# A two-layer decoder on one core: probabilities scaled in two steps, and half of the gate products as 7 block products in place of 8

## The chip, the cores and the metric

One core of a Trainium2 chip runs the whole program. The metric is the device time of one execution in microseconds (us); lower is better. The engines are called as in the profile: PE is TensorE (matmuls; its weight loads are listed apart as PEld), DVE is VectorE, ACT is ScalarE, POOL is GpSimd, SP is SyncE, which here only issues DMAs.

## What is computed

The program is a decoder of two layers on 512 rows of 1024 features, in float32. Each layer has an input projection, four attentions of four heads each (MoBA, FoX, MLA, dilated), an output projection, and a SwiGLU feed-forward part (FFN) of 2816 columns, with RMS norms around both. Cut to what the change touches:

```python
p = jax.nn.softmax(sc, axis=-1)
o = jnp.einsum('bhqk,bhkd->bhqd', p.astype(v.dtype), v)
...
f = jax.nn.silu(jnp.einsum('bsd,df->bsf', h, w_gate[l])) * jnp.einsum('bsd,df->bsf', h, w_up[l])
f = jnp.einsum('bsf,fd->bsd', f, w_down[l])
x = x + rmsnorm(f, g_post_ffn[l])
```

## The kernel before

**Precision.** A float32 operand goes to PE as a high part and a low part. ACT rounds the high part off (a cast), DVE subtracts it to get the low part; both together are called a split here. `mm3` (lines 196 to 199) makes one product of such operands with three matmuls, on lines 197, 198 and 199.

**Attention.** `attend` (line 438) is a generator for one unit: one head and the query tiles `qa` to `qb`, of 128 rows each. There are 20 units per layer, 12 with four query tiles (FoX, MLA, MoBA) and 8 with two (dilated). For each tile PE makes the scores (L454), DVE adds the mask and finds the row's extreme (L457), ACT takes the exponential and sums the row into `den` (L459, an ACTIVATE and then a short instruction that reads the sum out). After the last tile DVE inverts all sums (L462), and POOL multiplies each tile by its inverse (L465), from the shortest (128 columns) to the longest (512). Then PE transposes the scaled blocks (L474): the first bank that is filled takes one block of every query tile, so a unit with four tiles fills it only when the last tile is scaled. ACT and DVE split the transposed blocks (L476, L477), and PE multiplies them by the values (L482, L483). `weave` (line 397) interleaves the units with projection work, and begins the scores of the next unit before the current one is finished.

**FFN.** `ffn` (line 800) works through 22 column blocks of 128. Blocks 0 and 1 are done apart. From block 2 on, a gate block is 8 products of 128 by 128 weights with 512 columns of the transposed input, so 24 matmuls of 512 columns (`block`, L811), followed by SiLU on ACT (L928). At every odd block the up projection of two blocks is made by `two_blocks` (L891), which cuts weights and input in 2 by 2 blocks and forms the result from 7 products of blocks in place of 8 (Strassen's scheme in Winograd's form). Each of the 7 is 4 by 3 matmuls of 256 columns. The sums of input blocks are made once per layer (L843 to L866); the sums of weight blocks are made per pair: 4 `combine` (L882), 7 splits (L876, L877), 2 copies of a product out of PSUM (L901, L904) and 7 `add` (L894), all but the copies and casts on DVE. The up result goes to two scratch tiles, and DVE multiplies it onto the gate (L936).

**Order and buffers.** Every engine runs its instructions in order. The order is laid out when the program is built, by priority of program order and by a planner's costs; at run time engines wait for one another on semaphores. Split weights have 6 buffers (`WSPL`), raw weights 5 (`WRAW`), the sums of weight blocks 4 (tag `temp`). The 7 products of a pair take PSUM banks from four pools: 3 banks `ps_mm`, 2 `ps_s`, 2 `ps_t`, 1 `ps_o`. After the last pair the down projection (`ps_d`) fills all 8 banks.

Of the kernel before, what the change touches and what calls it, by code (L numbers as in the profile page):

```python
# [13 lines left out]
ALU = mybir.AluOpType  # L14
PSUM = bass.MemoryType.PSUM

P = 128
# [64 lines left out]
def decoder(ctx, tc, x, positions, w_in, b_forget, g_mla_q, w_mla_q_up, g_mla_kv, w_mla_kv_up,  # L82
            w_out, g_pre_mix, g_post_mix, w_gate, w_up, w_down, g_pre_ffn, g_post_ffn, consts, out):
    nc = tc.nc
# [10 lines left out]
    def bank(pool, name):  # L95
        return pool.tile([P, 512], F32, name=name, tag=pool.name)
# [10 lines left out]
    def H(name):  # L107
        return keep.tile([P, 512], F32, name=name, tag="part", bufs=NPART)
# [165 lines left out]
    def mixing(l, h_in, in_slots, out_slots, w_first):  # L274
# [110 lines left out]
        def attention(e0, tag, passes, vt, bias, spans, outer, more=None):  # L385
            units = [(h, sp) for sp in spans for h in range(4)] if outer else [(h, sp) for h in range(4) for sp in spans]
            return [(attend(e0, tag, h, sp[0], sp[1], passes, vt, bias, more), sum(sp) * (sp[1] - sp[0]) + sp[1], lambda h=h: h in passes)
                    for h, sp in units]
# [49 lines left out]
        def attend(e0, tag, h, qa, qb, passes, vt, bias, more):  # L438
# [4 lines left out]
            den = small.tile([P, nq], F32, name="den", tag="den", bufs=4)  # L443
            pr = keep.tile([P, PRW], F32, name="pr", tag="pr", bufs=2)
            offs = {}
            off = 0
            for qt in range(qa, qb):
# [5 lines left out]
                for i, (a, b) in enumerate(terms):  # L453
                    nc.tensor.matmul(ps[:, 0:w], a if a.shape[-1] == P else a[:, qt * P:(qt + 1) * P], b[:, 0:w],  # L454
                                     start=i == 0, stop=i == n - 1)
                p = pr[:, off:off + nk]
                nc.vector.tensor_tensor_reduce(p, ps[:, 0:nk], bias(h, qt, p), scale=-1.0, scalar=3e38,  # L457
                                               op0=ALU.add, op1=ALU.min, accum_out=neg[:, qt:qt + 1])
                nc.scalar.activation(p, p, AF.Exp, bias=neg[:, qt:qt + 1], scale=-1.0, accum_out=den[:, qt - qa:qt - qa + 1])  # L459
                offs[qt] = off  # L460
                off += nk
            nc.vector.reciprocal(den, den)  # L462
            for qt in range(qa, qb):
                p = pr[:, offs[qt]:offs[qt] + (qt + 1) * P]
                nc.gpsimd.tensor_scalar(p, p, den[:, qt - qa:qt - qa + 1], 1.0, op0=ALU.mult, op1=ALU.mult)  # L465
            yield
            ncol = (qb - qa) * P
            po = bank(ps_o, "ps_o")
# [331 lines left out]
    def ffn(l, xt, h, turns, f_slots, after):  # L800
        fq = []
# [4 lines left out]
        def w_of(src, j, into=(None, None)):  # L806
            cs = slice(j * P, (j + 1) * P)
            return [weights(src[l, 4 * i * P:4 * (i + 1) * P, cs].rearrange("(k p) c -> p k c", p=P), [4, P], into=into[i])
                    for i in range(2)]

        def block(ps, w, hs):  # L811
            for k in range(KD):
                hi, lo = w[k // 4]
                mm3(ps[:, hs], hi[:, k % 4, :], lo[:, k % 4, :], h[0][k // 4][:, k % 4, hs], h[1][k // 4][:, k % 4, hs],
                    k == 0, k == KD - 1)
# [52 lines left out]
        def raw_of(src, j, i):  # L868
            raw = wp.tile([P, 4, P], F32, name="wraw", tag="wraw", bufs=WRAW)
            nc.sync.dma_start(raw, src[l, 4 * i * P:4 * (i + 1) * P, j * P:(j + 1) * P].rearrange("(k p) c -> p k c", p=P))  # L870
            return raw

        def split_w(raw):
            hi = wp.tile([P, 4, P], F32R, name="whi", tag="whi", bufs=WSPL)
            lo = wp.tile([P, 4, P], F32R, name="wlo", tag="wlo", bufs=WSPL)
            nc.scalar.copy(hi, raw)  # L876
            nc.vector.tensor_tensor(lo, raw, f32(hi), op=ALU.subtract)  # L877
            return hi, lo

        def combine(a, b, op):  # L880
            s = T(F32, "wsum").rearrange("p (k c) -> p k c", c=P)
            nc.vector.tensor_tensor(s, a, b, op=op)  # L882
            return s

        def product(pool, w, n):
            ps = bank(pool, "ps_7")[:, 0:256]
            for k in range(4):
                mm3(ps, w[0][:, k, :], w[1][:, k, :], ops[n][0][k], ops[n][1][k], k == 0, k == 3)
            return ps

        def two_blocks(src, j, d1, d2):  # L891

            def add(to, a, b):
                nc.vector.tensor_tensor(to, a, b, op=ALU.add)  # L894

            c11, c12, c21, c22 = [d[:, s] for d in (d1, d2) for s in half]
            a11 = raw_of(src, j, 0)
            a21, a22 = raw_of(src, j + 1, 0), raw_of(src, j + 1, 1)
            a12 = raw_of(src, j, 1)
            p1 = product(ps_mm, split_w(a11), "11")  # L900
            nc.scalar.copy(c12, p1)  # L901
            s1 = combine(a21, a22, ALU.add)
            p5 = product(ps_s, split_w(s1), "T1")
            nc.scalar.copy(c22, p5)  # L904
            p2 = product(ps_o, split_w(a12), "21")
            add(c11, p2, c12)
            s2 = combine(s1, a11, ALU.subtract)
            p6 = product(ps_mm, split_w(s2), "T2")
            add(c12, p6, c12)
            s3 = combine(a11, a21, ALU.subtract)  # L910
            p7 = product(ps_t, split_w(s3), "T3")
            add(c21, p7, c12)
            s4 = combine(a12, s2, ALU.subtract)
            add(c12, c12, c22)
            add(c22, c22, c21)
            p3 = product(ps_s, split_w(s4), "22")
            add(c12, p3, c12)
            p4 = product(ps_t, split_w(a22), "T4")
            add(c21, p4, c21)

        for j in range(KF):
            if j < 2:
                (pg, _), (pu, _) = halves[2 * j:2 * j + 2]
            else:
                wg, pg = w_of(w_gate, j), bank(ps_mm, "ps_g")
                block(pg, wg, slice(0, 512))
            f = fq[j]
            nc.scalar.activation(f, pg, AF.Silu)  # L928
            if j < 2:
                nc.vector.tensor_tensor(f, f, pu, op=ALU.mult)  # L930
            elif j % 2 == 1:
                u = H("u1"), H("u2")
                two_blocks(w_up, j - 1, *u)
                for i in range(2):
                    f = fq[j - 1 + i]
                    nc.vector.tensor_tensor(f, f, u[i], op=ALU.mult)  # L936
# [53 lines left out]
    for c in range(2):  # L990
        pg = bank(ps_s, "gain")
# [5 lines left out]
    with tc.manual_schedule(engines={mybir.EngineType.Activation, mybir.EngineType.DVE, mybir.EngineType.Pool}):  # L997

        st, tr = {}, {}
        for o in "s0 a0 w0 w1 t0 s1 w2 w3 a1 s2 t1 a2 s3 t2 a3 t3".split():  # L1000
            t = int(o[1])
# [10 lines left out]
    for l in range(depth):  # L1012
        pool_share[0] = SHARE_MIX
        xt, h, turns = mixing(l, h, set_a, set_b, w_first if l == 0 else None)
        nxt = []

        def after(t):
            dst = out[0] if l + 1 == depth else x_mid[l]
            for c in range(2):
                nc.sync.dma_start(dst[t * P:(t + 1) * P, 512 * c:512 * c + 512], xt[t][c])  # L1020
            if l + 1 < depth:
                if not nxt:
                    nxt.append(gain(g_pre_mix, l + 1))
                    nxt.append(new_h(set_b))
                pre_norm(t, xt[t], nxt[0], nxt[1])

        ffn(l, xt, h, turns, set_a, after)
        if nxt:
            h = nxt[1]
        set_a, set_b = set_b, set_a  # L1030
# [21 lines left out]
```

## Time and profile before

| what | us |
|---|---|
| runs of the kernel before: median of three (lowest, highest) | 1266.09 (1265.72, 1267.85) |
| the profiled execution: its own time | 1268.2 |
| its span, first to last instruction | 1266.4 |
| PE busy in the span | 1228.6 (97%) |
| DVE busy | 821.4 (65%) |
| ACT busy | 646.4 (51%) |
| POOL busy | 225.5 (18%) |

The span is the time from the first instruction to the last; the profiled execution's own time holds 1.8 us more. In a row of the timeline the first number is the start, the second the duration; matmuls are pipelined, so what a matmul costs in a dense stream is the step from its start to the next start and not its listed duration. A bracket at the end of a row tells how long the engine was idle before it and what ended that.

### The profile page before, as it was taken

Reading aid. Unit: us, or ns where it says so; the run is one execution under the profiler, and the core shown is the slowest. Engines: PE = TensorE matmul, PEld = TensorE weight load, DVE = VectorE, ACT = ScalarE, POOL = GpSimd, SP = SyncE. Lnnn points to the kernel's source line nnn. Section 1 sums busy time; section 2 is a strip of 40 time slices with the busy share of each in tenths; the row PEclk is TensorE's granted clock in tenths of the full one; section 3 lists DMA queues with packets and bytes.
Section 4 is the critical chain, followed back from the end, with each engine's and each line's share of the span. In section 5 each row is a group of like instructions: output and inputs, shape, how many; then the busy total and the mean of one; then the engine's idle time right before and its main releaser. Section 6 shows DMA issues by size and latency. Waiting matters only on the chain.

```text
span 1266.4 us, 19777 instructions
## 1 busy us (share of the span) xinstructions
PE 1228.6 (97%) x7044; PEld 1063.4 (84%) x7044; DVE 821.4 (65%) x1621; ACT 646.4 (51%) x1403; POOL 225.5 (18%) x305
## 2 busy tenths in 40 slices
PE   8999999999999999999999999999899999999998
PEld 7878877779989898888788788778798989898886
DVE  6876866787766666533466668676787666674334
ACT  6676756754434344422456767667553434353332
POOL 3223334443000000000131324433430000000001
PEclk9999999989999999999999999999999999999999
DMA  7221241521433333433342222324224333334331
GB/s 230 72 60 42 66 116 55 172 68 34 127 99 107 93 109 92 125 100 100 125 117 73 59 56 70 100 88 137 68 64 126 95 108 97 105 100 123 94 93 75
DMA packets 158054, 121.60 MB, mean 96 GB/s; under 512 B 9090, under 2 KB 133122, under 8 KB 157956
## 3 DMA queue, kind: packets, MB, share of 16 engines
q1 hardware_dynamic: 151908, 111.55, 30.3%
q10 hardware_dynamic: 6048, 8.80, 2.6%
q8 instruction: 55, 0.90, 0.3%
q14 instruction: 43, 0.35, 0.1%
HBM read 111.93 MB, written 4.19 MB: 92 GB/s over the span
## 4 chain that ended last, share of the span: by engine, by line
PE 75%; DVE 4%; ACT 2%; POOL 2%; issue 2%; DMA 1%; DVEq 0%; POOLq 0%; ACTq 0%; SPq 0%
PE ps_g L198 6%; PE ps_g L197 6%; PE ps_g L199 6%; PE ps_d L197 6%; PE ps_d L199 6%; PE ps_d L198 6%; PE ps L197 5%; PE ps L199 5%; PE ps L198 5%; PE ps_s L454 2%; PE ps_out L199 2%; PE pT L474 2%; PE ps_out L198 2%; PE ps_out L197 2%; PE ps_qk L197 2%; PE ps_qk L198 2%
## 5 line engine op out<-in xcount | busy, mean ns | idle before, releaser
L173 DVE TENSOR_TENSOR wlo<-wraw,whi 128x512 fp32r<-128x512 f32 x249 | 179.9, 729 | 149.7 <-ACT whi L168 144.8
L168 ACT CAST whi<-wraw 128x512 fp32r<-128x512 f32 x268 | 163.9, 620 | 213.2 <-PE ps_d L199 121.0
L198 PE MATMUL ps_g<-h,whi 128*128 128x512 f32 (+1 forms) x384 | 144.2, 376 | 5.0 <-DVE h L231 5.0
L197 PE MATMUL ps_g<-h,whi 128*128 128x512 f32 (+1 forms) x384 | 143.9, 375 | 1.4 <-ACT h L231 1.2
L199 PE MATMUL ps_g<-h,wlo 128*128 128x512 f32 (+1 forms) x384 | 143.6, 374 | 0.0
L876 ACT CAST whi<-wsum 128x512 fp32r<-128x512 f32 x80 | 49.7, 622 | 149.4 <-PE ps_g L198 71.9
L240 POOL TENSOR_SCALAR rstd<-ssp 128x1 f32<-128x1 f32 x16 | 6.9, 433 | 647.8 <-ACT jk L236 647.7
L465 POOL TENSOR_SCALAR pr<-pr,den 128x128 f32<-128x128 f32 (+3 forms) x128 | 78.1, 629 | 192.1 <-DVE den L462 188.6
L197 PE MATMUL ps_d<-whi,fh 128*128 128x512 f32 x288 | 112.2, 390 | 0.0
L199 PE MATMUL ps_d<-whi,fl 128*128 128x512 f32 x288 | 112.1, 389 | 0.0
L198 PE MATMUL ps_d<-wlo,fh 128*128 128x512 f32 x288 | 112.0, 389 | 0.0
L877 DVE TENSOR_TENSOR wlo<-wsum,whi 128x512 fp32r<-128x512 f32 x80 | 54.9, 690 | 83.0 <-ACT whi L876 83.0
L197 PE MATMUL ps<-sum,whi 128*128 128x256 f32 x320 | 90.2, 282 | 0.0
L198 PE MATMUL ps<-sum,whi 128*128 128x256 f32 x320 | 90.1, 282 | 0.0
L199 PE MATMUL ps<-sum,wlo 128*128 128x256 f32 x320 | 90.1, 281 | 0.0
L198 PEld LDWEIGHTS ps_g<-h,whi 128*128 128x128 f32 x384 | 73.1, 190 | 18.0 <-DVE h L231 6.2
L197 PEld LDWEIGHTS ps_g<-h,whi 128*128 128x128 f32 x384 | 73.1, 190 | 14.5 <-ACT h L231 2.7
L199 PEld LDWEIGHTS ps_g<-h,wlo 128*128 128x128 f32 x384 | 73.2, 191 | 12.6
L197 PE MATMUL ps_qk<-h,whi 128*128 128x512 f32 x192 | 76.8, 400 | 0.0
L199 PE MATMUL ps_qk<-h,wlo 128*128 128x512 f32 x192 | 75.7, 394 | 0.0
L198 PE MATMUL ps_qk<-h,whi 128*128 128x512 f32 x192 | 75.7, 394 | 0.0
L459 ACT ACTIVATE pr<-pr,neg 128x128 f32<-128x128 f32 (+3 forms) x128 | 71.5, 560 | 5.9 <-DVE neg L457 4.9
(312 smaller groups left out, 3335.2 us busy)
## 6 DMA issues: line engine op xcount, KB each, us to landing
wraw<-in_w_gate_dram SPq DMA_DIRECT2D x88, 256.0 KB, 3.4
wraw<-in_w_up_dram SPq DMA_DIRECT2D x88, 256.0 KB, 3.1
wraw<-in_w_down_dram SPq DMA_DIRECT2D x88, 256.0 KB, 2.8
wraw<-in_w_in_dram SPq DMA_DIRECT2D x72, 256.0 KB, 3.0
wraw<-in_w_out_dram SPq DMA_DIRECT2D x32, 256.0 KB, 2.9
xt<-in_x_dram SPq DMA_DIRECT2D x16, 256.0 KB, 4.4
rope_b<-rope_a ACTq DMA_DIRECT2D x64, 64.0 KB, 2.0
wraw<-in_w_in_dram SPq DMA_DIRECT2D x16, 178.0 KB, 3.6
```

The costliest lines, as they stand in the source:

```text
L168: nc.scalar.copy(hi, raw)
L173: nc.vector.tensor_tensor(lo, raw, f32(hi), op=ALU.subtract)
L197: nc.tensor.matmul(ps, a_hi, b_hi, start=start, stop=False)
L198: nc.tensor.matmul(ps, a_hi, b_lo, start=False, stop=False)
L199: last_mm[0] = nc.tensor.matmul(ps, a_lo, b_hi, start=False, stop=stop)
L240: nc.gpsimd.tensor_scalar(r, ss[:, 0:1], ss[:, 1:2], EPS, op0=ALU.add, op1=ALU.add)
L454: nc.tensor.matmul(ps[:, 0:w], a if a.shape[-1] == P else a[:, qt * P:(qt + 1) * P], b[:, 0:w], start=i == 0, stop=i == n - 1)
L459: nc.scalar.activation(p, p, AF.Exp, bias=neg[:, qt:qt + 1], scale=-1.0, accum_out=den[:, qt - qa:qt - qa + 1])
L465: nc.gpsimd.tensor_scalar(p, p, den[:, qt - qa:qt - qa + 1], 1.0, op0=ALU.mult, op1=ALU.mult)
L474: nc.tensor.transpose(pt[:, i * P:(i + 1) * P], pr[:, offs[qt] + kt * P:offs[qt] + (kt + 1) * P], ident)
L876: nc.scalar.copy(hi, raw)
L877: nc.vector.tensor_tensor(lo, raw, f32(hi), op=ALU.subtract)
```

## The change

Two edits. In `attend` the inverse and the scaling are done in two steps: after the exponential of the last but one tile for all tiles so far, and after that of the last tile for the last one. In `ffn` the gate blocks of the pairs that begin at 4, 8, 12, 16 and 20, so 5 of the 10 pairs of a layer, are made by `two_blocks`, straight into the tiles `fq[j]` and `fq[j + 1]`, where SiLU then works in place.

```diff
@@ attend
                 offs[qt] = off
                 off += nk
-            nc.vector.reciprocal(den, den)
-            for qt in range(qa, qb):
-                p = pr[:, offs[qt]:offs[qt] + (qt + 1) * P]
-                nc.gpsimd.tensor_scalar(p, p, den[:, qt - qa:qt - qa + 1], 1.0, op0=ALU.mult, op1=ALU.mult)
+
+                if qt >= qb - 2:
+                    new = range(qa, qt + 1) if qt == qb - 2 else [qt]
+                    d = den[:, new[0] - qa:qt - qa + 1]
+                    nc.vector.reciprocal(d, d)
+                    for t in new:
+                        p = pr[:, offs[t]:offs[t] + (t + 1) * P]
+                        nc.gpsimd.tensor_scalar(p, p, den[:, t - qa:t - qa + 1], 1.0, op0=ALU.mult, op1=ALU.mult)
             yield
@@ ffn
             if j < 2:
                 (pg, _), (pu, _) = halves[2 * j:2 * j + 2]
+            elif j - j % 2 in (4, 8, 12, 16, 20):
+                if j % 2 == 0:
+                    two_blocks(w_gate, j, fq[j], fq[j + 1])
+                pg = fq[j]
             else:
                 wg, pg = w_of(w_gate, j), bank(ps_mm, "ps_g")
                 block(pg, wg, slice(0, 512))
```

## Rows read from the trace of the kernel before

**Rows 1.** The page: span and busy time of the engines.

```profile
span 1266.4 us, 19777 instructions
PE 1228.6 (97%) x7044; PEld 1063.4 (84%) x7044; DVE 821.4 (65%) x1621; ACT 646.4 (51%) x1403; POOL 225.5 (18%) x305
```

**Rows 2.** Busy time by stretch: attention of layer 0, gate and up of both layers.

```profile
core 0: us, PE busy (x) PEld busy (x) DVE busy (x) ACT busy (x) POOL busy (x), PEclk, DMA share, GB/s
110.00:160.00 50.00, 47.77 (x311) 41.56 (x309) 38.69 (x88) 35.48 (x84) 19.93 (x25) 1.00 0.28 77
306.00:515.10 209.10, 209.10 (x1322) 190.24 (x1321) 144.69 (x253) 88.40 (x160) 4.23 (x3) 1.00 0.36 103
935.00:1140.00 205.00, 205.00 (x1303) 186.83 (x1303) 141.84 (x249) 87.73 (x158) 2.27 (x2) 1.00 0.36 102
```

**Rows 3.** Timeline of PE where gate (ps_g) and up (ps) change over.

```profile
316.93 0.28 PE L197 MATMUL ps<-h,whi 128*128 128x256 f32 x1
...
326.94 0.39 PE L197 MATMUL ps_g<-h,whi 128*128 128x512 f32 x1
...
337.84 0.28 PE L197 MATMUL ps<-h,whi 128*128 128x256 f32 x1
```

**Rows 4.** Timeline of DVE where it works without a pause.

```profile
367.55 0.42 DVE L894 TENSOR_TENSOR u<-u 128x256 f32<-128x256 f32 x1
367.88 0.42 DVE L894 TENSOR_TENSOR u<-ps,u 128x256 f32<-128x256 f32 x1
368.21 0.68 DVE L877 TENSOR_TENSOR wlo<-wraw,whi 128x512 fp32r<-128x512 f32 x1
368.82 0.68 DVE L936 TENSOR_TENSOR f<-f,u 128x512 f32<-128x512 f32 x1
369.42 0.41 DVE L894 TENSOR_TENSOR u<-ps,u 128x256 f32<-128x256 f32 x1
369.75 0.68 DVE L882 TENSOR_TENSOR wsum<-wraw 128x512 f32<-128x512 f32 x1
```

**Rows 5.** Busy time in one stretch, columns as in rows 2.

```profile
323.80:326.94 3.14, 3.14 (x29) 3.14 (x28) 3.11 (x8) 1.35 (x3) 0.00 (x0) 1.00 0.88 243
```

**Rows 6.** Waits in gate and up of layer 0: total us, times, longest.

```profile
ACT whi L876 <- PE ps_g L198: 38.6, 25, 2.1
DVE wlo L173 <- ACT whi L168: 6.7, 9, 0.8
DVE u L894 <- PE ps L199: 4.5, 24, 0.2
```

**Rows 7.** Groups of instructions in gate and up of layer 0: busy us, mean ns.

```profile
L876 ACT CAST whi<-wsum 128x512 fp32r<-128x512 f32 x40 | 24.9, 622 | 75.3 <-PE ps_g L198 36.5 <-DVE wsum L882 25.9 <-issue 12.8
L928 ACT ACTIVATE f<-ps_g 128x512 f32<-128x512 f32 x21 | 12.5, 593 | 0.0
```

**Rows 8.** Waits of the whole span for probabilities and their sums.

```profile
PE pT L474 <- POOL pr L465: 7.2, 15, 0.9
DVE den L462 <- ACT pr L459: 8.7, 14, 1.0
```

**Rows 9.** Timeline of one unit's scaling and of the transposes behind it.

```profile
155.75 3.46 POOL L465 TENSOR_SCALAR pr<-pr,den 128x128 f32<-128x128 f32 x4 [8.92 <-DVE den L462]
157.16 0.33 PE L474 MATMUL pT<-cst,pr 128*128 128x128 f32 x1
158.04 0.33 PE L474 MATMUL pT<-cst,pr 128*128 128x128 f32 x1 [0.56 <-POOL pr L465]
158.60 0.33 PE L474 MATMUL pT<-cst,pr 128*128 128x128 f32 x1 [0.23 <-POOL pr L465]
159.27 0.66 PE L474 MATMUL pT<-cst,pr 128*128 128x128 f32 x4 [0.34 <-POOL pr L465]
```

**Rows 10.** Scaling of four tiles elsewhere, and all inverses (ns: least, median, most).

```profile
93.21 2.06 POOL L465 TENSOR_SCALAR pr<-pr,den 128x128 f32<-128x128 f32 x4 [13.93 <-DVE den L462]
L462 DVE RECIPROCAL den<-den x40: 151/172/179, 71.7 to 872.8; 128x4 f32<-128x4 f32 x24, 128x2 f32<-128x2 f32 x16
```

## Prediction

> **What bounds the kernel now.** I read the busy times first. PE is busy for 97% of the span and no other engine for more than 65% [rows 1], so only what takes time off PE, or out of its gaps, shortens the kernel. The busy times by stretch then tell the two edits apart. In gate and up of both layers PE is busy without any gap, 209.10 us of 209.10 and 205.00 of 205.00, at full clock; DVE is at 69% [rows 2]. There only fewer or shorter matmuls help. In the attention stretch PE is busy for 47.77 us of 50, DVE for 38.69 [rows 2]; there is a gap of some 4%, and one part of it is time in which the transposes wait for the scaled probabilities [rows 8].
>
> **The gate products.** I call an ordinary gate pair G, an up pair U, and a gate pair by 7 products G*. The timeline of PE has U from 316.93 to 326.94, so 84 matmuls of 256 columns in 10.01 us, 0.1192 each; and G from 326.94 to 337.84, so 48 matmuls of 512 columns in 10.90 us, 0.2271 each [rows 3]. G* issues what U issues, so I take U's 10.01 us for it. That is 12.5% fewer columns but only 8.2% less time, since two short matmuls take 5% longer than a long one. One pair saves 0.89 us, and 5 pairs in each of 2 layers save **8.9 us**, all of it on the path, since PE has no gaps there.
>
> This row and a rule of the skill disagree. The Trainium skill, page "TensorE: Matmul & The Clock Gate", section "Back-to-back issue gap", gives the isolated gap as columns over 2.4 plus 2.5 ns, from which I estimate 215.8 and 109.2 ns, 1.19 us per pair and 11.9 us in all. The trace's 227.1 and 119.2 ns do not agree with it.
>
> What G* adds beside PE: DVE does 7 splits, 4 sums of weights and 7 adds in place of 4 splits. Back to back, DVE starts a new instruction 0.605 us after one of 512 columns and 0.335 after one of 256 [rows 4]. G* therefore costs 11 x 0.605 + 7 x 0.335 = 9.0 us of DVE where G costs 2.4; U with its two multiplications costs 10.2. Per two pairs the order is now G, U, G*, U: DVE 31.8 us, PE 40.9, 78%. But in U, G*, U it is 29.4 us in 30.0 of PE, 98%, and DVE also waits: an add for the end of its product, 4.5 us in 24 times, 0.19 each [rows 6], so about 4 us for 21 adds. Then DVE falls 3.4 us behind in such a stretch. The cover is the 6 buffers of split weights: the casts of ACT wait for PE to give a buffer back (38.6 us in 25 times) [rows 6], so splits run 6 products ahead, 6 x 1.43 = 8.6 us; in the next G DVE has 10.9 us for 2.4 of work and catches up. The nearest evidence that a full DVE does not stop PE is a stretch before the change: DVE busy 3.11 us of 3.14, PE 3.14 [rows 5]. ACT has room: 9 casts or copies and 2 SiLUs, by 622 and 593 ns [rows 7], are 6.8 us of 10.0. PSUM has room too: with these four pools no product meets a bank that was filled fewer than 7 products before, so an add may come 8 us late. The same weights are loaded; the SP queue only issues those of the second block before the first block's second half. At the end of a layer DVE goes from U, G*, U straight into the splits for the down projection, whose first matmuls need the banks of the last products. The trace has no such end; between nothing and the 3.4 us of lag I take 0.4 us per layer, near nothing, because the buffers cover 8.6 us. **Sum of this edit: -8.9 + 0.8 = -8.1 us.**
>
> **The scaling.** Now POOL starts when all four exponentials are done, and takes 2.06 us [rows 10] to 3.46 us [rows 9] for four tiles; the transposes of the first bank wait for it. After the change three of them are under way while the fourth exponential runs, and only the last and longest stays behind. In the unit shown, PE starts its transposes at 157.16 and then waits 0.56, 0.23 and 0.34 us, 1.13 named; from start to start it takes 2.11 us for three steps that need about 0.11 each (the four behind them end 0.66 after the first begins, one alone 0.33), so 1.8 is lost [rows 9]. One tile begun at 155.75 would be done by about 157, and the whole 1.8 goes. Over the span PE waits 7.2 us in 15 times for these tiles [rows 8]; by the unit's ratio of 1.8 to 1.13 up to 11.4 us are lost. The edit gives between 0 and 11.4. I take **-4.5 us**, below the named 7.2: where the wait goes, the split of the transposed block or the next scores come late instead, in units with two tiles only the smaller of two scalings moves, and the planner lays the order anew.
>
> The price is a second inverse per unit, 40 more of about 0.172 us [rows 10], 6.9 us on DVE. The first of the two is a new wait: on DVE's queue it stands until ACT has read out the last but one sum, and behind it are the mask of the last tile and splits of weights; ACT's last exponential, and so POOL and the transposes, wait for that mask. Today the inverse waits 8.7 us in 14 of 40 times [rows 8]; twice that, and the 6.9, is 16 us of a DVE that has 11 us free in 50 [rows 2], spread over 40 units. I cost it at nothing, with DVE's free time as its cover; if half of the added wait reached PE it would be 4.4 us.
>
> **The sum** stands against the profiled execution's 1268.2 us: -8.1 - 4.5 = -12.6, so 1255.6. The median of the runs is 2.1 us lower, so I predict **1253.5**.
>
> **The rivals.**
>
> *Only the gate edit counts.* The transposes find another wait, or the new one costs what the old one gave: the edit in `attend` gives between 0 and +4.4. For it: PE has only a 4% gap there, of many small kinds [rows 2]. Against it: the named waits. Time 1258.0 to 1262.4.
>
> *DVE uses up part of the lead.* If the planned order puts the new sums late, PE stops for half of what it gained, some 0.45 us per G*: -4.5 - 4.5 + 0.8, so 1257.9 with the scaling's gain, 1262.4 without.
>
> *Slower: DVE becomes the bound in U, G*, U.* If the lead of 6 splits is not there, because splits of the next pair stand in the queue behind adds of the current one, the 3.4 us by which DVE falls behind land on PE in each of 10 stretches: +34 - 8.9 - 4.5, so 1287. It turns the sign of the gate edit once more than 0.89 us per stretch is not covered. For it: 98% before any wait. Against it: the full DVE that did not stop PE [rows 5], the casts that wait for PE [rows 6], the lead of 8.6 us and the G in between.
>
> *Shorter matmuls cost less than U shows.* By the isolated gap the gate edit would give 3.0 us more than by the rows: 1250.5. The row against it is the same instruction in the same stage [rows 3].
>
> **How the numbers follow.** Forecast (1248 to 1257) 58%, only the gate edit 22%, part of the lead 8%, slower 8%, shorter matmuls 2%, and 2% for a smaller mishap that ends near no change. The range is 1248 to 1262.5: its lower end is the full 8.9 with a scaling near the upper bound (9.2 of 11.4), its upper end takes in the first two rivals. A measurement can tell 0.2% from no change, so faster is below 1263.6 and slower above 1268.6. Faster: 58 + 22 + 8 + 2, less 8 for ends of these cases that reach past 1263.6, is 82%; same 9%; slower 9%.
>
> **What would show it.** Right: the gate and up stretch shorter by some 4.5 us per layer, PE busy in it without a gap, 0.119 us from start to start in G*; DVE busy near all of U, G*, U, with casts of ACT still waiting for PE; transposes that wait for POOL in fewer and shorter times, of 2 us in all or less. Wrong: PE waiting for splits in U, G*, U or at the first down products; a wait of the transposes for something new of the same size; more than 0.12 us per short matmul.

## The result and the profile after

The changed kernel takes 1253.91 us (median, 1252.15 to 1254.13), the kernel before in the same comparison 1266.97; the ratio is 0.9891, with a 95% interval from 0.9878 to 0.9904. The forecast was 1253.5. One execution of a later kernel (nine pairs by 7 products) took 6701.93 us where its other four took 1274.77 to 1277.87; no run here explains it, its trace is not read, and that kernel's ratio leaves it out. The page of the changed kernel, to lay beside [rows 1]:

```profile
span 1252.0 us, 20776 instructions
PE 1218.8 (97%) x7404; PEld 1075.3 (86%) x7404; DVE 888.2 (71%) x1801; ACT 667.4 (53%) x1453; POOL 219.5 (18%) x305
```

PE has 360 matmuls more (10 pairs by 84 less 48) and is still busy for less time; DVE has 66.8 us more to do. Where the 14.4 us between the two spans lie is read from the starts of PE's groups in the timelines:

| stretch, by the start of PE's groups | before | after | difference |
|---|---|---|---|
| first scores to first gate matmul, layer 0 | 216.1 | 212.2 | -3.9 |
| the same, layer 1 | 213.2 | 209.7 | -3.5 |
| first gate matmul to first up pair, layer 0 | 41.6 | 41.4 | -0.2 |
| the same, layer 1 | 40.0 | 41.4 | +1.5 |
| first up pair to first down matmul, layer 0 | 198.2 | 193.6 | -4.5 |
| the same, layer 1 | 198.2 | 193.6 | -4.5 |
| all other stretches together | 259.2 | 260.0 | +0.8 |

Gate and up give 9.1 us, the attention 7.4. The 1.5 us in the fourth row is a matter of the clock, told of at the end.

Gate and up, busy time by stretch (columns as in [rows 2]); PE has no gap after the change either, and DVE rose from 69% to 85%:

```profile
302.10:506.70 204.60, 204.60 (x1503) 195.16 (x1502) 174.76 (x323) 99.09 (x185) 4.24 (x3) 1.00 0.36 105
921.00:1125.00 204.00, 204.00 (x1498) 194.58 (x1497) 174.03 (x322) 99.11 (x185) 4.22 (x3) 1.00 0.36 105
```

The timeline of PE where the first U meets the first G*, where the U behind it meets a G, and where the last one meets the down projection:

```profile
322.94 0.28 PE L199 MATMUL ps<-sum,wlo 128*128 128x256 f32 x1
323.05 0.28 PE L197 MATMUL ps<-h,whi 128*128 128x256 f32 x1
...
342.94 0.28 PE L199 MATMUL ps<-sum,wlo 128*128 128x256 f32 x1
343.05 0.39 PE L197 MATMUL ps_g<-h,whi 128*128 128x512 f32 x1
...
506.56 0.28 PE L199 MATMUL ps<-sum,wlo 128*128 128x256 f32 x1
506.68 0.39 PE L197 MATMUL ps_d<-whi,fh 128*128 128x512 f32 x1
```

No step is longer than the 0.12 us of a dense stream, at any of the three. From 323.05 to 343.05 a G* and a U take 20.00 us. Busy time block by block, over the next G, U, G* and U:

```profile
343.05:353.94 10.89, 10.89 (x50) 9.01 (x49) 7.54 (x14) 3.38 (x6) 0.00 (x0) 1.00 0.42 116
353.94:363.96 10.02, 10.02 (x86) 10.01 (x84) 7.15 (x13) 5.38 (x10) 0.00 (x0) 1.00 0.43 123
363.96:373.96 10.00, 10.00 (x87) 10.00 (x85) 10.00 (x21) 4.89 (x9) 0.00 (x0) 1.00 0.23 66
373.96:383.96 10.00, 10.00 (x87) 10.00 (x85) 9.21 (x20) 5.62 (x11) 0.00 (x0) 1.00 0.52 149
```

During G* DVE is busy for 10.00 us of 10.00 and PE does not notice. The waits in this stretch of layer 0 (us in total, times, longest) tell how:

```profile
ACT whi L880 <- PE ps L198: 27.7, 37, 0.9
ACT whi L880 <- PE ps_g L198: 14.4, 10, 2.1
DVE wsum L886 <- DMA wraw<-in_w_gate_dram: 10.2, 5, 3.0
DVE wsum L886 <- DMA wraw<-in_w_up_dram: 4.7, 5, 1.7
DVE u L898 <- PE ps L199: 2.1, 12, 0.2
```

The casts still wait for PE to give split buffers back, so the splits still run ahead. DVE's own waits are not those that I had counted: the adds wait 2.1 us in all, but the sums of weight blocks wait 14.9 us for their loads.

How far the splits run ahead can be read from the two timelines, since DVE makes the splits in the order in which PE uses them. The end of a split is compared with the start of the first matmul that reads its low part (L199). In the last U, G*, U of layer 0, where G* begins at 486.68:

```profile
483.19 0.69 DVE L881 TENSOR_TENSOR wlo<-wraw,whi 128x512 fp32r<-128x512 f32 x1
487.58 1.28 DVE L944 TENSOR_TENSOR f<-f,u 128x512 f32<-128x512 f32 x2
488.78 0.68 DVE L881 TENSOR_TENSOR wlo<-wsum,whi 128x512 fp32r<-128x512 f32 x1
...
489.78 0.28 PE L199 MATMUL ps<-h,wlo 128*128 128x256 f32 x1
492.66 0.28 PE L199 MATMUL ps<-sum,wlo 128*128 128x256 f32 x1
```

The first of these splits is done 5.9 us ahead of its matmul, the other, two products later, 3.2 us. Ahead of the second, from 485.72 to 488.78, DVE makes no split, but one sum, the last adds of the U and its two multiplications (L944). At the end of the stretch the lead is 5.4 us again. In the last three stretches of the layer it is 2.5, 3.1 and 3.2 us at the least; in the first two, which begin with less, 0.8 and 0.9.

In the attention the wait of PE's transposes for POOL fell from the 7.2 us of [rows 8] to 3.4:

```profile
PE pT L478 <- POOL pr L469: 3.4, 7, 1.0
```

The unit that answers to [rows 9], in the timeline, on DVE, POOL and PE:

```profile
153.09 0.17 DVE L466 RECIPROCAL den<-den 128x3 f32<-128x3 f32 x1
153.42 3.64 POOL L469 TENSOR_SCALAR pr<-pr,den 128x128 f32<-128x128 f32 x4 [7.97 <-PE ps_v L199]
154.08 0.15 DVE L466 RECIPROCAL den<-den 128x1 f32<-128x1 f32 x1
155.62 0.59 PE L478 MATMUL pT<-cst,pr 128*128 128x128 f32 x2
156.44 0.33 PE L478 MATMUL pT<-cst,pr 128*128 128x128 f32 x1 [0.23 <-POOL pr L469]
```

Here POOL begins 2.2 us ahead of PE's first transpose, where it was 1.4 before. But the four scalings are one run of 3.64 us, so the third and fourth block still come late: the edit brought the work forward by the time between two inverses, which is 1.0 us here.

### The profile page after: what moved, and what is told of

Its sections match the earlier page's. It is cut to its first block, busy times and chain, and to the rows that moved or that the text cites. A ratio compares the mean times of both kernels' runs of the same rounds, so it can differ in the third digit from the quotient of the medians.

```text
span 1252.0 us, 20776 instructions
## 1 busy us (share of the span) xinstructions
PE 1218.8 (97%) x7404; PEld 1075.3 (86%) x7404; DVE 888.2 (71%) x1801; ACT 667.4 (53%) x1453; POOL 219.5 (18%) x305
## 4 chain that ended last, share of the span: by engine, by line
PE 82%; DVE 6%; ACT 4%; DMA 3%; issue 2%; POOL 2%; ACTq 0%; SPq 0%; DVEq 0%; POOLq 0%
PE ps L197 8%; PE ps L199 8%; PE ps L198 8%; PE ps_d L197 6%; PE ps_d L198 6%; PE ps_d L199 6%; PE ps_g L198 4%; PE ps_g L197 3%; PE ps_g L199 3%; PE ps_s L454 3%; PE ps_qk L197 2%; PE ps_qk L199 2%; PE ps_qk L198 2%; PE pT L478 2%; PE ps_out L199 1%
## 5 line engine op out<-in xcount | busy, mean ns | idle before, releaser
L168 ACT CAST whi<-wraw 128x512 fp32r<-128x512 f32 (+1 forms) x228 | 138.5, 620 | 177.2 <-PE ps_d L199 121.0
L197 PE MATMUL ps<-sum,whi 128*128 128x256 f32 x480 | 135.3, 282 | 0.0
L198 PE MATMUL ps<-sum,whi 128*128 128x256 f32 x480 | 135.2, 282 | 0.0
L199 PE MATMUL ps<-sum,wlo 128*128 128x256 f32 x480 | 135.1, 281 | 0.0
L199 PE MATMUL ps_d<-whi,fl 128*128 128x512 f32 x288 | 112.1, 389 | 0.0
L199 PE MATMUL ps<-h,wlo 128*128 128x256 f32 x360 | 101.8, 283 | 0.0
L197 PE MATMUL ps<-h,whi 128*128 128x256 f32 x360 | 101.7, 282 | 0.0
L198 PE MATMUL ps<-h,whi 128*128 128x256 f32 x360 | 101.6, 282 | 0.0
L197 PEld LDWEIGHTS ps<-sum,whi 128*128 128x128 f32 x480 | 91.8, 191 | 0.0
L198 PEld LDWEIGHTS ps<-sum,whi 128*128 128x128 f32 x480 | 91.8, 191 | 0.0
L199 PEld LDWEIGHTS ps<-sum,wlo 128*128 128x128 f32 x480 | 91.7, 191 | 0.0
L198 PE MATMUL ps_g<-h,whi 128*128 128x512 f32 (+1 forms) x224 | 81.5, 364 | 5.8 <-DVE h L231 5.8
L197 PE MATMUL ps_g<-h,whi 128*128 128x512 f32 (+1 forms) x224 | 81.3, 363 | 1.0 <-ACT h L231 1.0
L199 PE MATMUL ps_g<-h,wlo 128*128 128x512 f32 (+1 forms) x224 | 81.0, 362 | 0.0
L880 ACT CAST whi<-wraw 128x512 fp32r<-128x512 f32 x90 | 55.8, 619 | 40.8 <-PE ps L198 28.1
```

The source lines that it names most:

```text
L197: nc.tensor.matmul(ps, a_hi, b_hi, start=start, stop=False)
L198: nc.tensor.matmul(ps, a_hi, b_lo, start=False, stop=False)
L199: last_mm[0] = nc.tensor.matmul(ps, a_lo, b_hi, start=False, stop=stop)
```

## Experiments

All ratios are against the kernel before, with their 95% intervals. Times of stretches are between starts of PE's groups in the timelines, as in the table above. The diffs of the second inverse and of the inverse that nobody reads stand against the kernel before, which has no gate edit; the others against the changed kernel, unless it is said.

### One edit at a time

The gate edit alone, that is the changed kernel with the old lines in `attend`:

```diff
-                if qt >= qb - 2:
-                    ...
+            nc.vector.reciprocal(den, den)
+            for qt in range(qa, qb):
+                ...
```

> The changed kernel with the scaling of before: only the gate edit. Theory (the two edits add up, the gate edit is worth its shorter matmuls): 10 pairs by 0.91 us, so 9 us less than the kernel before, about 1257.5 us, with the gate and up stretch at 193.6 us from the first up matmul to the first down matmul, as in the changed kernel. Rival (the edits need each other, or most of the gain is the planner's new order in attention): 3 us or less gained, about 1263.

Measured: 1257.36 us against 1265.45, ratio 0.9933 (0.9919 to 0.9946). From the first up pair to the first down matmul it takes 193.6 us in each layer, as the changed kernel does.

The scaling edit alone, without the branch in `ffn`:

```diff
-            elif j - j % 2 in (4, 8, 12, 16, 20):
-                ...
```

> The kernel before with the scaling in two steps alone. Theory: the stretch from the first scores to the first gate matmul gets shorter by 3.9 us in layer 0 and 3.5 in layer 1 as in the changed kernel, and 1.5 us of it is given back between the mixing and the first up product of layer 1, so some 5 us in all, about 1261.5 us; PE waits for POOL ahead of the transposes for 3.4 us in place of 7.2. Rival (the gain in attention comes with the FFN edit's other order): within 1.5 us of the kernel before.

Measured: 1261.11 us, ratio 0.9962 (0.9949 to 0.9974). First scores to first gate matmul: 211.7 and 210.7 us. PE waits for POOL ahead of the transposes for 4.4 us in 8 times.

The two give 8.1 and 4.3 us by the medians, 12.4 together, and the changed kernel 13.1: the edits add up. The attention of the gate-only kernel, which has the scaling of before, takes 215.1 and 212.5 us, 1.6 less than in the profile of before. So of the 7.4 us in the table about 1.6 may be the difference between two executions. Over all the traces, this stretch takes 426.2 to 429.3 us in the two layers together in the four kernels with the scaling of before, and 420.6 to 422.7 in the seven with two steps, 5.7 less in the mean. The edit is worth 4 to 6 us.

### What the scaling edit gains, and what it costs

The inverse in two steps, but all scalings written after the second:

```diff
+                if qt >= qb - 2:
+                    d = den[:, 0 if qt == qb - 2 else qt - qa:qt - qa + 1]
+                    nc.vector.reciprocal(d, d)
-            nc.vector.reciprocal(den, den)
             for qt in range(qa, qb):
```

> The kernel before with the inverse taken in two steps, but all scalings still after the second: the price of the scaling edit without its gain. Theory (DVE's free time covers 40 more inverses and their wait): within 1 us of the kernel before. Rival (the new wait on DVE's queue reaches the mask of the last tile and then PE): 3 to 4.4 us slower, about 1270.

Measured: 1260.35 us, ratio 0.9959 (0.9947 to 0.9972), as fast as with the scalings moved. I had expected the price without the gain, and the experiment did not test that: in its trace POOL starts the first three scalings as soon as the first inverse is done (at 70.46, 0.28 us after the inverse began at 70.18), since the planner orders by what is ready:

```profile
70.46 1.40 POOL L468 TENSOR_SCALAR pr<-pr,den 128x128 f32<-128x128 f32 x3 [18.07 <-DVE den L465]
```

The place of the scalings in the text does nothing that can be told; the second inverse is the whole edit.

So the price was measured with an inverse that nobody reads, while the scaling keeps waiting for the one over all tiles:

```diff
+                if qt == qb - 2:
+                    spare = small.tile([P, nq], F32, name="spare", tag="spare", bufs=4)
+                    nc.vector.reciprocal(spare[:, 0:nq - 1], den[:, 0:nq - 1])
             nc.vector.reciprocal(den, den)
```

> The kernel before with one spare inverse more per unit, taken of the sums of all but the last tile into a tile that nobody reads; the inverse that counts and the scaling stay as before, after the last tile. It has the price of the scaling edit (40 inverses and a wait on DVE's queue each) and, since the scaling needs the later inverse, none of its gain. Theory (the price is nothing, so the gain of the two-step kernels is the earlier start of the scaling, wherever in the program the scalings stand): within 1.5 us of the kernel before. Rival (the gain came from the other order that one more instruction makes the planner lay out): 3 us or more faster. Third: 3 to 4.4 us slower, the price reaches PE.

Measured: 1264.83 us against 1265.76, ratio 0.9993 (0.9984 to 1.0002): no change that can be told. The 40 inverses and their wait cost nothing that can be told. Nor is the gain of the two-step kernels mainly the planner's other order: of their 4.3 and 5.1 us at most 2.0 fit into this interval. The wait for POOL in its trace lies between the old one (7.2 us in 15 times) and that of the scaling edit alone (4.4 in 8):

```profile
PE pT L477 <- POOL pr L468: 5.1, 13, 0.9
```

Then more of the same, every tile inverted and scaled as soon as its own exponential is done:

```diff
-                if qt >= qb - 2:
-                    ...
+                d = den[:, qt - qa:qt - qa + 1]
+                nc.vector.reciprocal(d, d)
+                nc.gpsimd.tensor_scalar(p, p, d, 1.0, op0=ALU.mult, op1=ALU.mult)
```

> The changed kernel with each tile inverted and scaled as soon as its own exponential is done (for units of four tiles four steps in place of two; units of two tiles are unchanged). Theory (what is late behind the transposes is the last tile alone, and the other three are done in time anyway): within 1.5 us of the changed kernel, the wait of the transposes for POOL stays near 3 us. Rival (POOL is still behind with the first three when the last comes): 2 us or more faster.

Measured: 1248.49 us, ratio 0.9868 (0.9852 to 0.9885). This is the lowest median of the study. The wait of PE's transposes for POOL fell again:

```profile
PE pT L474 <- POOL pr L465: 1.7, 5, 0.6
```

In the unit above, the timeline of POOL has its work spread out ahead of the transposes:

```profile
151.15 0.94 POOL L465 TENSOR_SCALAR pr<-pr,den 128x128 f32<-128x128 f32 x2 [6.33 <-DVE den L464]
152.74 0.59 POOL L465 TENSOR_SCALAR pr<-pr,den 128x384 f32<-128x384 f32 x1 [0.66 <-DVE den L464]
154.04 1.57 POOL L465 TENSOR_SCALAR pr<-pr,den 128x512 f32<-128x512 f32 x1 [0.70 <-DVE den L464]
```

My theory that only the last tile is late does not hold in the unit of the changed kernel, where the first three were late as well, and the wait here is half of that kernel's. Whether this gives more time than the change is not shown. Its attention takes 420.3 us in the two layers against 421.9, 1.6 us less, and the seven kernels with two steps differ among themselves by 2.2; another 3.0 us of its profile are two stretches in which its clock happened not to fall (the last section), and the intervals of the two ratios overlap.

### Is the lead of 6 splits what covers a full DVE?

Three, then four, of the six pairs of split buffers are held by idle tiles from the first two blocks to the last up pair, `n` being 3 or 4; the third kernel is the one of before with four held:

```diff
+        held = [wp.tile([P, 4, P], F32R, name="held", tag=tag, bufs=WSPL) for _ in range(n) for tag in ("whi", "wlo")]
+        for z in held:
+            nc.gpsimd.memset(f32(z[:, 0, 0:1]), 0.0)
         for j in range(KF):
...
+        for z in held:
+            nc.gpsimd.tensor_tensor(f32(z[:, 0, 0:1]), f32(z[:, 0, 0:1]), fq[KF - 1][:, 0:1], op=ALU.add)
         tail = 4
```

> The changed kernel, with 3 of the 6 pairs of buffers for split weights held by idle tiles from the first two blocks to the end of the last up pair, so that splits run 3 products ahead and not 6. Theory (the cover against a full DVE is these buffers, and DVE falls behind by up to 3.4 us): 3 products are 4.3 us, from which a cast, a subtraction and their hand-overs take 1.7; PE begins to stop in up, gate by 7, up; 2 to 10 us slower than the changed kernel. Rival (the lead does not matter, DVE simply keeps up): within 1 us of it.

> The changed kernel with 4 of the 6 pairs of buffers held, so a lead of 2 products, 2.9 us less 1.7 us of cast and subtraction. Theory: PE stops at most products in which DVE is behind; 10 us or more slower than the changed kernel, and it loses more than the kernel before does with the same buffers held. Rival: within 1 us.

> The kernel before with 4 of the 6 pairs of buffers held in the same way. Its up pairs alone fill DVE too (10.2 us in 10.0), but an ordinary gate pair stands between them. Theory: it loses less than half of what the changed kernel loses with the same buffers, 2 to 8 us, and the gain of the change is turned into a loss. Rival (both lose the same, the change stays some 9 us ahead).

| kernel | us | ratio (interval) | first up pair to first down matmul, layers 0 and 1 |
|---|---|---|---|
| before | 1265.70 | | 198.2, 198.2 |
| changed | 1253.91 | 0.9891 (0.9878 to 0.9904) | 193.6, 193.6 |
| changed, lead 3 | 1257.61 | 0.9933 (0.9917 to 0.9950) | 194.3, 195.1 |
| changed, lead 2 | 1298.30 | 1.0255 (1.0240 to 1.0270) | 209.5, 209.1 |
| before, lead 2 | 1286.30 | 1.0164 (1.0149 to 1.0179) | 200.8, 200.6 |

The whole times also hold the 6 to 8 us per layer that lead 2 costs at the first gate blocks, which want six buffers at once, in either kernel; the last column is what counts. There lead 3 costs the changed kernel 2.1 us, lead 2 costs it 31.3 us and the kernel before 5.1. So the change needs these buffers, and half of them would nearly do. Read as above, a split of G* in layer 0 is done at most 5.9 us ahead with six pairs, 1.7 with three and 0.9 with two. With lead 2 the change is slower than what it replaced. But this run does not test a full DVE, as I had meant it to: DVE is busy for 163.9 of the 209.5 us and itself waits 29.0 us for casts, which wait for PE to give a buffer back. PE's waits there are for the cast that cannot start earlier:

```profile
PE ps L197 <- ACT whi L880: 6.3, 16, 0.5
```

### Without the G in between: nine pairs by 7 products

```diff
-            elif j - j % 2 in (4, 8, 12, 16, 20):
+            elif j - j % 2 >= 4:
```

> The changed kernel with all gate pairs from 4 on, so 9 of 10 in place of 5, made by 7 products. DVE then needs 19.2 us in every 20.0 of PE, with no ordinary gate pair in between to catch up. Theory (the lead of 6 splits covers a stretch of 30 us, but DVE at 96% plus its waits for products and loads, some 2 to 4 us in 20, falls behind for good): the lead is used up after three to five pairs, PE then stops, and the 8 further pairs give less than half of their 7.3 us, so between 1249 and 1255. Rival (once behind, DVE never waits, and 96% is enough): all of it, 7.3 us less than the changed kernel, about 1246.6.

Measured: 1276.59 us, ratio 1.0083 (1.0069 to 1.0096), slower than the kernel before and some 21 us above the range in which I had put it. For a trace it was run once more:

> Nine gate pairs by 7 products once more, for its trace. Theory (DVE is the bound once the lead is used up): DVE busy for more than 97% of every gate by 7 and up pair after the first two, PE less than 90%, no wait of ACT's casts for PE, and 22 to 23 us for the two in place of 20.0. Rival (something else stops PE: loads, banks, the queue order): DVE idle for more than 10% there.

Measured, in a single run: 1271.96 us. Busy time in two periods of U and G*, 21.2 us each, then behind PE's longest stop and a little later (the number behind the engines is the granted clock):

```profile
433.20:454.40 21.20, 20.26 (x168) 20.06 (x168) 19.09 (x39) 10.40 (x21) 0.00 (x0) 1.00 0.35 100
454.40:475.60 21.20, 20.16 (x168) 20.05 (x168) 19.36 (x39) 10.23 (x21) 0.00 (x0) 1.00 0.35 101
...
391.40:394.70 3.30, 3.30 (x15) 3.30 (x16) 3.30 (x7) 0.62 (x1) 0.00 (x0) 0.50 0.28 79
396.00:399.30 3.30, 3.30 (x30) 3.30 (x30) 3.01 (x8) 1.06 (x3) 0.00 (x0) 1.00 0.59 170
```

The waits of layer 0 in this stretch:

```profile
PE ps L199 <- DVE wlo L881: 7.7, 8, 2.0
DVE wsum L886 <- DMA wraw<-in_w_up_dram: 12.3, 8, 2.0
DVE wsum L886 <- DMA wraw<-in_w_gate_dram: 3.4, 7, 1.0
```

The timeline of PE at that stop:

```profile
389.07 0.28 PE L198 MATMUL ps<-sum,whi 128*128 128x256 f32 x1
391.39 0.58 PE L199 MATMUL ps<-sum,wlo 128*128 128x256 f32 x1 [2.04 <-DVE wlo L881]
391.77 0.41 PE L197 MATMUL ps<-sum,whi 128*128 128x256 f32 x1
391.99 0.41 PE L198 MATMUL ps<-sum,whi 128*128 128x256 f32 x1
```

PE runs dense until 348.5, 37 us into the stretch, and then stops once in nearly every period, always for a split by DVE. The lead never fills: after the first product the splits are done 3.2 us ahead at the most up to that stop, and 3.4 afterwards, but for 4.5 behind the longest stop. Most periods are some 21.2 us: DVE's 19.2 us of work and near 2 us in which DVE itself waits, mostly for loads. My expectation missed on every figure: DVE is at 90 to 91%, not 97%, PE at 95 to 96%, not under 90%, and the casts still wait for PE, 35.5 us in 40 times. DVE's idle share is near the 10% that I had given to the rival, and its waits for loads are part of what that rival named. The price is higher than the stops, because after one of 2 us the clock is at half for 3.3 us. The stretch takes 202.0 and 202.7 us in the two layers against 193.6.

If DVE's work is the cause, taking some away should help. Two of the four sums of each pair went to POOL, which is idle there:

```diff
-            s3 = combine(a11, a21, ALU.subtract)
+            s3 = combine(a11, a21, ALU.subtract, nc.gpsimd)
...
-            s4 = combine(a12, s2, ALU.subtract)
+            s4 = combine(a12, s2, ALU.subtract, nc.gpsimd)
```

> Nine gate pairs by 7 products, with the third and fourth sum of weight blocks of every pair made by POOL in place of DVE. DVE then needs 16.8 us in 20.0. Theory (DVE's work is what stops the nine pairs): PE is dense again and the 8 further pairs give their 7.3 us, so about 1246.6 us. Rival (POOL's sums are late or slow DVE down, or DVE was not the cause): 1260 us or more.

Measured: 1337.96 us, ratio 1.0572 (1.0558 to 1.0587), far slower. The waits of SP's queue in layer 0:

```profile
SPq L874 <- POOL wsum L886: 132.1, 16, 9.8
```

The timeline, DVE first and then POOL at the same time:

```profile
434.31 1.43 DVE L881 TENSOR_TENSOR wlo<-wsum,whi 128x512 fp32r<-128x512 f32 x1
436.00 1.45 DVE L881 TENSOR_TENSOR wlo<-wraw,whi 128x512 fp32r<-128x512 f32 x1
440.38 0.69 DVE L886 TENSOR_TENSOR wsum<-wraw 128x512 f32<-128x512 f32 x1 [2.93 <-DMA wraw<-in_w_gate_dram]
...
432.33 2.87 POOL L886 TENSOR_TENSOR wsum<-wraw 128x512 f32<-128x512 f32 x1 [9.04 <-DVE wlo L881]
435.16 1.74 POOL L886 TENSOR_TENSOR wsum<-wraw,wsum 128x512 f32<-128x512 f32 x1
```

A sum that took DVE 0.605 us takes POOL 1.7 to 2.9, and two splits of DVE beside it 1.43 and 1.45 instead of 0.68 (not all: over the run the splits take 0.78 and 1.03 us in the mean, by their source). Worse, the sums on POOL wait for a free tile and come late; raw weights are released late, their loads start late (132 us of SP's waiting in the layer), and DVE then stands before the next sum for 2.93 us. This run says nothing for or against DVE's work as the cause, since it made the loads worse.

The last run gave the loads a sixth buffer, in a kernel with nine pairs and with each tile scaled by itself. The room came from small tiles of the attention (`angn`, `kn` and `t4` put into scratch tiles, `qr` and `t1` with one buffer for two), which may cost a little there:

```diff
-            elif j - j % 2 in (4, 8, 12, 16, 20):
+            elif j - j % 2 >= 4:
...
-NR, NTMP, NPART, WRAW, WSPL = 12, 4, 2, 5, 6
+NR, NTMP, NPART, WRAW, WSPL = 12, 4, 2, 6, 6
```

> Nine gate pairs by 7 products, each tile scaled by itself, and a sixth buffer for raw weights (room for it made by letting a few small tables of the attention share other tiles). In the nine pairs with five buffers DVE worked 19.2 us for two pairs and waited some 2 more in its queue for loads, since a raw weight buffer comes free only when DVE has used it, and a period became 21.1 us. Theory (those waits for loads are what tips DVE over the 20.0 us of PE): with a sixth buffer the loads start earlier, the waits go, PE is dense again, and the 8 further pairs give their 7.3 us on top of the kernel with each tile scaled by itself, about 1241 us. Rival (DVE at 96% falls behind anyway, by the order in its queue): the wait for loads shrinks but PE still stops; 1255 us or more.

Measured: 1272.18 us (1265.19 to 1275.07 in ten runs), ratio 1.0045 (1.0028 to 1.0062). The theory falls. Busy time in a stretch of 20 us:

```profile
440.00:460.00 20.00, 19.88 (x167) 19.59 (x166) 18.77 (x38) 9.79 (x20) 0.00 (x0) 1.00 0.37 106
```

The waits of layer 0:

```profile
DVE wsum L882 <- DMA wraw<-in_w_up_dram: 9.3, 9, 1.7
PE ps_d L197 <- DVE u L894: 3.6, 2, 1.8
PE ps L199 <- DVE wlo L877: 1.9, 4, 0.9
```

The waits for loads shrink (those for the up weights from 12.3 us to 9.3), a period in layer 0 falls to some 20.7 us, and PE's stops for the splits of layer 0 from 7.7 us to 1.9. The stretch takes 198.0 and 201.9 us, less than without the sixth buffer and still more than the 193.6 of five pairs. DVE is late at the end of layer 0 too: the first down matmuls wait twice for the adds that empty their banks, 3.6 us, and the way from the first down matmul to the next layer takes 130.1 us instead of the changed kernel's 125.5, again with a clock that fell (0.65 from 506.4 to 516.0). What a seventh buffer would do is open; there was no room for one. So loads are a part of what stops the nine pairs. That the rest is DVE's load and the order in its queue is argued from the traces; no run took work from DVE without making the loads worse.

## Why the prediction was right, point by point

**The gate products: right in mechanism and size.** G* takes U's time, 10.00 us for 10.01 forecast. The stretch is 4.54 us shorter per layer, 0.91 per pair for 0.89. The rows decided rightly: by the isolated gap of the Trainium skill (page "TensorE: Matmul & The Clock Gate", section "Back-to-back issue gap") G* would take an estimated 9.17 us, and no trace of this study shows that.

**The 0.8 us for the ends of the layers: not there.** The first down matmul follows without a gap. Without these 0.8 us the sum for this edit would have been 8.9, against 9.1 in the trace and 8.1 by the medians, so the medians cannot tell.

**DVE in U, G*, U: the lag about right, for a wrong reason, which is luck.** I had DVE at work for 29.4 us of 30.0 and 4 us of waits of the adds. In the three windows shown it is busy for 26.4 of 30.0, 88%, full only in G*: part of the U's splits is made in the G before, where DVE is busy for 7.54 us in place of 2.4. All adds of a layer wait 2.1 us. I put the loads at nothing, "the SP queue only issues those of the second block before the first block's second half"; the sums wait 14.9 us per layer for them, 7.7 of it while PE is in a G. A raw buffer comes free only when DVE has used it, so a full DVE delays its own loads. In the last stretch, where the loads cost DVE 0.2 us, what takes from the lead is the order in DVE's queue: the last adds and the multiplications of the U stand ahead of the splits of G*. The lead falls there, and in the two stretches before, by 2.7 to 3.4 us, and I had forecast 3.4.

**The lead as cover: right, but shorter than I said.** It is 5.9 us ahead of G* and not 8.6: by the traces a cast waits for PE to end the product whose buffer it takes, so the product at work counts among the six, and the cast and the subtraction come on top. Three pairs of buffers lose 2.1 us in two layers. In layer 0 the closest split is 0.8 us ahead, in the first stretch.

**The rival in which DVE becomes the bound** is real, and so is the condition that I gave: splits do stand in the queue behind the adds of the current pair. In the changed kernel that takes about half of the lead, and the next G gives it back. With nine pairs there is no G in between, and PE stops after 37 us.

**The scaling: 4.5 us forecast, 4.3 by the medians.** The picture behind it was too simple. I had three scalings done while the fourth exponential runs, and all of the 1.8 us of the unit shown gone; there the first inverse comes only 1.0 us before the second and the scalings still run for 3.64 us. So 3.4 us of waits stay, where I had said 2 or less. That the 4.5 fits all the same is in part luck: I had taken 6.9 off the upper bound of 11.4 for other reasons, and the traces put the edit at 5.7 in the mean. The price of nothing for 40 inverses was right (the 16 us of DVE named there are the 6.9 and the added 8.7).

## What to carry to other kernels

A scheme that trades a dense engine's work for another engine's is worth what the stretch gives, not the operation count: 12.5% fewer columns were 8.2% less time, and only while the other engine's average load, with its own waits for loads, leaves it behind for no longer than the buffers reach. Alternating the scheme with ordinary blocks is what kept this one within its buffers; doing it everywhere turned a gain of 1% into a loss. And where a planner orders by readiness, an early start comes from cutting the dependency, here one inverse into several, and not from moving lines.

## What the runs showed of the hardware that I had not expected

**The clock at the head of the FFN.** From the first gate matmul to the first up pair a layer takes either about 40.0 us or 41.4 to 41.6, in every kernel with six free pairs of split buffers and five raw buffers. The granted clock goes with it. The same stretch in the kernel before (layer 0 and layer 1):

```profile
275.35:317.35 42.00, 39.70 (x260) 36.89 (x261) 33.64 (x45) 18.58 (x38) 15.77 (x17) 0.92 0.14 40
901.90:943.90 42.00, 38.95 (x274) 36.10 (x275) 35.30 (x48) 18.62 (x38) 15.82 (x17) 1.00 0.14 39
```

PE waits there for the normed input, 1.9 us at the longest, before dense work begins, and in some executions the clock falls for a while (0.50 from 280 to 284 us in the first row's stretch). The profile of before has it in one layer, that of the changed kernel in both, and that of the kernel with each tile scaled by itself in none. It is worth 1.5 us each time, which is more than some of the effects in this study, so two profiles are compared by stretch and not by span. In the nine pairs a stop of 2.0 us was followed by 3.3 us at 0.50, which is 1.2 of 2.4 GHz, with 0.213 us from start to start instead of 0.119.

**POOL and DVE on two inputs each.** In the run with sums on POOL two splits of DVE, which read two tiles each, took 1.43 and 1.45 us beside a sum on POOL, and 0.68 without one. The Trainium skill, page "GPSIMD Engine Reference", section "8. Key points", says that GpSimd shares its SBUF interfaces with VectorE and that they contend when a VectorE instruction has two SBUF inputs. The trace agrees, but not every split was slowed: two that began at 432.77, beside the sum on POOL of 2.87 us, took 1.28 us together.
